# Dilated attention in a fused decoder trunk: far keys handled class by class, shorter score blocks, and a reordered state-space output

## The chip, the cores and the metric

The kernel runs on one core of one Trainium2 chip. The metric is the device time of one execution in microseconds (us). The kernel before took 2345.99 us, the median of three runs from 2345.98 to 2347.3. The profiled execution, from which all rows below come, took 2347.55 us; its span from the first to the last instruction is 2345.70 us.

## The reference

Two layers of a decoder trunk on a sequence of 1024 tokens and 1024 features, all in float32. Layer 0 mixes tokens with a diagonal state-space model (S5) and a gated linear unit, layer 1 with dilated attention; each is followed by a SwiGLU feed-forward block. The change touches the S5 output and the attention of layer 1:

```python
DIL_PATTERNS = ((128, 1), (512, 4), (2048, 16))     # (window, dilation); 16 heads of 64
def dilated_mixer(xn, w_qkv, w_o, cos, sin):
    q, k, v = ...                                    # projections; rotary on the first 16 of 64
    for window, dilation in DIL_PATTERNS:
        o, l = dilated_branch(q, k, v, window, dilation)   # softmax over keys at distance d,
        ...                                          # 0 <= d <= window, d % dilation == 0
    w = jax.nn.softmax(jnp.stack(lses, axis=0), axis=0)
    o = jnp.einsum('gbsh,gbshd->bshd', w, jnp.stack(outs, axis=0))
    return o.reshape(bsz, seq, D_MODEL) @ w_o
```

The three branches, joined by their softmax denominators, are the same as one causal softmax in which a key at distance d has the weight c(d), the number of patterns that contain d: every d up to 128 counts once, a multiple of 4 up to 512 once more, a multiple of 16 up to 2048 once more. Both kernels use this form. A key with c = 0 takes no part, so beyond distance 128 only keys of the query's own class mod 4 matter, and beyond 512 only those at a multiple of 16.

## The kernel before, in words

All large products are done three times over, as high part times high part, low times high and high times low, with float32r operands (`mm3`, L243 to L246). The stages follow one another: S5 and its gate, feed-forward of layer 0, attention, its output projection, feed-forward of layer 1.

In the attention stage the 16 heads are taken as 8 pairs. For each pair `qk_pair` projects queries and keys (8 token tiles, 24 matmuls of 128x256 each), `rope` turns them on GpSimd, and 128x128 transposes (L1358) bring them to the layout features by tokens, as `QH`, `QL`, `KH`, `KL`, with one head on partitions 0 to 63 and the other on 64 to 127. `v_group` projects the values of two pairs. `unit(p, gq, ...)` does the attention of the 256 queries of group gq of pair p, as two blocks of 128 queries:

- Scores (L1402). Block i is multiplied with all keys from 0 to its end, 128(i+1) keys, in steps of at most 512. Each step is three products for each of the two heads; the two heads use different halves of the array's rows.
- Mask and maximum (L1419). VectorE adds `lc`, a table with 8 log c(d) or minus infinity, and takes the row maximum; ScalarE then takes the exponential in place with the row sum into `den` (L1430).
- Product with the values. For each block of 128 keys: 4 transposes of the weights (L1448), ScalarE copies them as `ph`, VectorE makes the rest `pl` (L1461), and L1480 multiplies both with the values into `po`. The step at the diagonal has one query block (2 transposes) only.
- ScalarE and VectorE add the two halves of `po` into the tile `o` (L1504).

`finish` takes the reciprocal of `den`, spreads and transposes it for each half of the tokens (4 transposes L1528), multiplies `o`, splits it and stores it for the output projection.

The order of all instructions is laid down by a planner, the class `Steps`. Each op has an engine, a cost in us, a due time, ops that it depends on, and slots that it takes and gives back ("sc": 2 score banks, "pt": 2, "po": 2, "t2": 4 tiles for `ph` and `pl`, "z" and "s": large tiles). It walks through time and gives each free engine the ready op that is due first. The hardware then runs each engine's queue in that order, held only by semaphores. For the seventh pair (p = 7) there is nothing left to project; parts of the output projection (`opart`, L244 to L246 into `po_`) are put in between where their banks are free.

In S5, `y_ops` (eight times, t = 0 to 7) adds in two PSUM banks `Y[0]` and `Y[1]` first 16 products of 128 rows (L741), then 32 products of 64 rows (L745): all of the lower row half (e = 0), then all of the upper (e = 1).

Of the kernel before, what the change touches and what calls it, by code (L numbers as in the profile page):

```python
# [39 lines left out]
SL = 12.0  # L40
# [30 lines left out]
def shape_constants():  # L71
    ident = np.eye(128, dtype=np.float32)
    i16 = np.tile(np.eye(16, dtype=np.float32), (8, 1))
    p = np.arange(128)[:, None]
    u = np.arange(1024)[None, :]
    delta = p + 896 - u
    c = ((delta >= 0) & (delta <= 128)).astype(np.float64)
    c += (delta >= 0) & (delta % 4 == 0) & (delta <= 512)
    c += (delta >= 0) & (delta % 16 == 0) & (delta <= 2048)
    lc = np.where(c > 0, 8.0 * np.log(np.maximum(c, 1.0)), NEG).astype(np.float32)  # L80
    inv = (np.float32(ROPE_THETA) ** (-np.arange(0, 16, 2, dtype=np.float32) / np.float32(16))).astype(np.float32)
    inv = np.broadcast_to(inv[None, :], (128, 8))
    return {"cst": np.ascontiguousarray(np.concatenate([ident, i16, inv], axis=1)), "lc": lc}
# [87 lines left out]
def trunk(tc, a, out):  # L171
# [39 lines left out]
    cst = const.tile([128, 152], F32, name="cst")  # L211
    ident, i16, inv = cst[:, 0:128], cst[:, 128:144], cst[:, 144:152]
    vec = const.tile([128, 56], F32, name="vec")
# [518 lines left out]
    def y_ops(t, at_, sd_, us, gs, tdep):  # L732
# [3 lines left out]
        def mm():  # L736
# [5 lines left out]
            for e in range(2):  # L742
                for q in range(4):
                    for ri in range(2):
# [9 lines left out]
        o = op("pe", 5.2, at_, mm, sd_ + tdep, take=["ey"], give=["b", "b", "b", f"sst{pb}"])  # L754
# [465 lines left out]
    sch = Steps({"z": 14, "s": 6, "nat": 2, "t2": 4, "tx": 2, "raw": 2, "w": 3, "sc": 2, "pt": 2, "po": 2, "qk": 2, "mx": 6}, ids={"s": [0, 0, 0, 0, 1, 1]})  # L1220
# [106 lines left out]
    def qk_pair(p, a0, a1):  # L1327
# [9 lines left out]
        for hf in range(2):  # L1337
            evs = []
            for tau in range(4 * hf, 4 * hf + 4):
# [8 lines left out]
                evs.append(op(ACT_, c_act(256, 1, 1), at_ + span, ev, [l, rso], take=["nat"] if tau % 4 == 0 else [], give=[t["bank"]]))  # L1348
# [26 lines left out]

    def unit(p, gq, a_s, a_t, a_e, last, pair):
# [6 lines left out]
        if "den" not in pair:  # L1383
            pair["den"] = am.tile([128, 2, 8], F32, tag="den", name=uid("den"), bufs=2)
        blk = [{}, {}]
        exps = []
        for b in range(2):
            i = 2 * gq + b
            n = 128 * (i + 1)
            wide = n > 512  # L1390
            t = blk[b]
            t["s"], t["mx"] = [None, None], [None, None]
            ms_ = [[], []]
            for c0 in range(0, n, 512):
                w = min(512, n - c0)

                def sc(t=t, i=i, c0=c0, w=w):
                    t[c0] = [bank(psc, "sc") for _ in range(2)]
                    qs = slice(128 * i, 128 * i + 128)
# [4 lines left out]
                o = op(PE_, max(0.64, 0.00135 * w), a_s + 0.01 * b, sc, qdeps, take=["sc", "sc"],  # L1404
                       give=["z"] * 4 if last and b == 1 and c0 + w == n else [], chain="sc")
                lasts["sc"] = o
                for h in range(2):
                    def mask(t=t, n=n, i=i, c0=c0, w=w, h=h, wide=wide):
                        if c0 == 0:
                            if wide or h == 0:  # L1410
                                tl = Z4("s_") if sch.got["s"] else B4("s_")
                                if not wide:
                                    t["s"] = [half(tl, 0), half(tl, 1)]
                                else:
                                    t["s"][h] = tl
                            t["mx"][h] = am.tile([128, 3], F32, tag="mx", name=uid("mx"), bufs=6)
                        mx = t["mx"][h]
                        l0 = 896 - 128 * i + c0
                        V.tensor_tensor_reduce(t["s"][h][:, c0:c0 + w], t[c0][h][:, 0:w], lc[:, l0:l0 + w], op0=ALU.add, op1=ALU.max,  # L1419
                                               scale=1.0, scalar=-3.0e38, accum_out=mx[:, c0 // 512:c0 // 512 + 1])  # L1420
                        if n <= 512:
                            V.tensor_scalar(mx[:, 2:3], mx[:, 0:1], -0.125, None, op0=ALU.mult)
                        elif c0:
                            V.tensor_scalar(mx[:, 2:3], mx[:, 0:1], mx[:, 1:2], -0.125, op0=ALU.max, op1=ALU.mult)
                    tk = (["mx"] + (["s"] if wide or h == 0 else [])) if c0 == 0 else []
                    ms_[h].append(op(DVE_, c_dve(w) + (0.15 if c0 + w == n else 0), a_s + 0.5, mask, [o] + ms_[h][-1:],
                                     take=tk, give=["sc"], chain="mask"))
            for h in range(2):
                def ex(t=t, n=n, i=i, h=h):
# [336 lines left out]
```

## Time and profile before

| what | value |
|---|---|
| median of three runs | 2345.99 us |
| profiled execution | 2347.55 us |
| its span | 2345.70 us |
| TensorE (PE) busy | 2255.6 us, 96% |
| VectorE (DVE) busy | 1482.9 us, 63% |
| ScalarE (ACT) busy | 962.4 us, 41% |
| GpSimd (POOL) busy | 761.0 us, 32% |
| bytes moved | 185.73 MB, mean 79 GB/s |

A busy share says how long at least one instruction of the engine was under way. Matmuls overlap: one of 256 columns is shown with 0.28 us, but the next one starts 0.12 us after it. What a matmul costs in a full queue is therefore read from start to start in the timeline, not from its duration.

### The profile page before, as it was taken

What the parts mean: (1) busy time and instruction counts of PE and PEld (TensorE: products, weight loads), DVE (VectorE), ACT (ScalarE), POOL (GpSimd) and SP (SyncE); (2) the same over time, 40 slices, a digit from 0 to 9 for tenths busy, and PEclk for the clock granted to TensorE, in tenths of its full rate; (3) what the DMA queues carried; (4) which work ended last, traced back from release to release, by engine and by line L of the source; (5) the groups of instructions that cost most, each with busy time, mean ns of one, the idle gap of its engine ahead of it and who ended that gap; (6) DMA issues with size and microseconds to landing.
All of it is one profiled execution on the core that took longest, in us unless ns stands there. A gap on an engine that the chain in (4) does not pass through costs nothing.

```text
span 2345.7 us, 32083 instructions
## 1 busy us (share of the span) xinstructions
PE 2255.6 (96%) x12424; PEld 1908.7 (81%) x12424; DVE 1482.9 (63%) x2463; ACT 962.4 (41%) x1845; POOL 761.0 (32%) x620
## 2 busy tenths in 40 slices
PE   4779999999999999999999999989999999999998
PEld 3667888888888888889999999968788888888887
DVE  9994357866666535355676666675976667763434
ACT  7522334333322324245565656554533333332333
POOL 6661226665565301031112121011454444430100
PEclk9879999999999999999999999999999999999999
DMA  5212322222221512120111010142222222153112
GB/s 144 85 51 67 107 89 65 83 88 82 88 83 54 224 54 81 46 72 28 37 46 37 28 55 28 55 135 82 72 91 89 91 81 81 54 185 138 46 54 90
DMA packets 203931, 185.73 MB, mean 79 GB/s; under 512 B 18697, under 2 KB 171521, under 8 KB 203778
## 3 DMA queue, kind: packets, MB, share of 16 engines
q1 hardware_dynamic: 201762, 176.34, 23.4%
q0 software_dynamic: 2016, 7.34, 0.9%
q8 instruction: 98, 1.61, 0.3%
q14 instruction: 55, 0.45, 0.1%
HBM read 141.71 MB, written 41.94 MB: 78 GB/s over the span
## 4 chain that ended last, share of the span: by engine, by line
PE 87%; DVE 7%; ACT 2%; DMA 1%; POOL 1%; issue 1%; SPq 0%; POOLq 0%; DVEq 0%; ACTq 0%
PE pT L246 7%; PE pT L245 7%; PE pT L244 7%; PE pB L245 5%; PE pB L244 5%; PE pB L246 5%; PE pqk L244 4%; PE pqk L246 4%; PE pqk L245 4%; PE fin L244 3%; PE fin L245 3%; PE fin L246 3%; PE po L1480 3%; PE dn L244 3%; PE dn L245 3%; PE dn L246 3%
## 5 line engine op out<-in xcount | busy, mean ns | idle before, releaser
L244 PE MATMUL pqk<-whi,hh 128*128 128x256 f32 x768 | 228.4, 297 | 0.4 <-ACT nat L1346 0.4
L246 PE MATMUL pqk<-whi,hl 128*128 128x256 f32 x768 | 217.0, 283 | 0.8 <-DVE hl L1105 0.8
L245 PE MATMUL pqk<-wlo,hh 128*128 128x256 f32 x768 | 217.0, 283 | 0.0
L246 PE MATMUL pT<-T,S 128*128 128x512 f32 x528 | 205.7, 390 | 0.9 <-DVE S L990 0.9
L244 PE MATMUL pT<-T,S 128*128 128x512 f32 x528 | 205.9, 390 | 0.6 <-ACT T L209 0.5
L245 PE MATMUL pT<-T,S 128*128 128x512 f32 x528 | 205.8, 390 | 0.4 <-DVE T L895 0.4
L1085 DVE TENSOR_TENSOR dwl<-wraw,dwh 128x512 fp32r<-128x512 f32 x86 | 64.5, 754 | 216.7 <-ACT dwh L209 206.8
L990 DVE TENSOR_TENSOR A<-wraw,A 128x512 fp32r<-128x512 f32 x132 | 139.4, 1068 | 77.1 <-ACT A L209 76.5
L209 ACT ACTIVATE dwh<-wraw 128x512 fp32r<-128x512 f32 x86 | 53.6, 629 | 265.4 <-PE dn L245 133.9
L244 PEld LDWEIGHTS pqk<-whi,hh 128*128 128x128 f32 x768 | 146.4, 191 | 9.9 <-issue 8.1
L246 PEld LDWEIGHTS pqk<-whi,hl 128*128 128x128 f32 x768 | 146.3, 191 | 1.0 <-DVE hl L1105 1.0
L1461 DVE TENSOR_TENSOR pl<-ptp,ph 128x512 fp32r<-128x512 f32 (+1 forms) x160 | 100.1, 634 | 74.2 <-ACT ph L209 73.4
L245 PEld LDWEIGHTS pqk<-wlo,hh 128*128 128x128 f32 x768 | 146.7, 191 | 0.0
L244 PE MATMUL pB<-B,A 128*128 128x512 f32 x352 | 137.5, 391 | 0.0
L245 PE MATMUL pB<-B,A 128*128 128x512 f32 x352 | 137.2, 390 | 0.0
L246 PE MATMUL pB<-B,A 128*128 128x512 f32 x352 | 137.1, 390 | 0.0
L245 PE MATMUL dn<-sl,dwh 128*128 128x512 f32 x352 | 136.7, 389 | 0.0
L244 PE MATMUL dn<-sh,dwh 128*128 128x512 f32 x352 | 135.5, 390 | 1.0 <-DVE dtmp L1099 1.0
L246 PE MATMUL dn<-sh,dwl 128*128 128x512 f32 x352 | 134.8, 389 | 0.0
L245 PE MATMUL fin<-dwl,sh 128*128 128x512 f32 x336 | 130.8, 389 | 0.0
L209 ACT ACTIVATE A<-wraw 128x512 fp32r<-128x512 f32 x132 | 80.4, 624 | 120.8 <-DMA wraw<-in_ffn_w_gate_up_dram 72.8
L246 PE MATMUL fin<-dwh,sl 128*128 128x512 f32 x336 | 129.7, 389 | 0.0
(1137 smaller groups left out, 6221.3 us busy)
## 6 DMA issues: line engine op xcount, KB each, us to landing
wraw<-in_ffn_w_gate_up_dram SPq DMA_DIRECT2D x88, 512.0 KB, 3.9
wraw<-in_ffn_w_down_dram SPq DMA_DIRECT2D x44, 512.0 KB, 3.3
hidd<-hid SPq DMA_DIRECT2D x32, 512.0 KB, 2.8
hd<-hidd SPq DMA_DIRECT2D x32, 512.0 KB, 8.9
wraw<-in_s_w_glu_dram SPq DMA_DIRECT2D x16, 512.0 KB, 4.0
wraw<-in_dil_w_qkv_dram SPq DMA_DIRECT2D x32, 256.0 KB, 3.3
x<-in_x_dram SPq DMA_DIRECT2D x8, 512.0 KB, 7.3
xts<-xT SPq DMA_DIRECT2D x8, 512.0 KB, 3.3
```

The lines of the kernel that those rows point to most:

```text
L209: A.activation(o, i, AF.Copy)
L244: T.matmul(ps, lh, rh, start=first, stop=False)
L245: T.matmul(ps, lh, rl, start=False, stop=False)
L246: T.matmul(ps, ll, rh, start=False, stop=last)
L990: V.tensor_sub(half(t, 1), src, half(t, 0).bitcast(F32))
L1085: V.tensor_sub(wl, half(raw, i), wh.bitcast(F32))
L1461: V.tensor_sub(o_, i_, (t["ph"][:, :, 1] if part else t["ph"]).bitcast(F32))
L1480: T.matmul(o_, l_, r_[:, h, cs], start=x == 0 and n_ == 0, stop=x == len(js) - 1 and n_ == len(todo) - 1)
```

## The change

Attention, in `unit`: blocks 4 to 7 (the second half of the tokens) get near keys only. `first_key` gives the first key block, 0 for blocks 0 to 3, 3 for block 4 and 4 for blocks 5 to 7. So the blocks have 128, 256, 384, 512, 256, 256, 384 and 512 keys. The two blocks of a group share one score step when both together have at most 512 keys (groups 0 and 2). The steps of the value product are `[0, 1]`, `[0, 1, 3, 2]`, `[4, 3, 5]` and `[4, 5, 7, 6]`; in groups 0 and 2 the first step's low part is multiplied last ("held").

A new function `far` handles, for each pair, the 512 queries of the second half with the keys of the first half at a distance over 128: in four classes mod 4, 128 queries by 128 keys each. Queries and keys of a class are read with a stride of 4 elements. The values are gathered by class with 8 DMAs from GpSimd's queue. The far part has a maximum and a sum of its own; `join` spreads them from class order to token order with one matmul, and finds the factors for both parts; `finish` then scales both parts of the second half and adds them. The due times share out the same 49 us per pair among five parts instead of four, the "z" slots go from 14 to 15 and the "s" slots from 6 to 5. The evacuations of the projections (L1346) stay in order (a chain).

S5, in `y_ops`: the 32 products of L745 alternate between the two row halves, and their planned cost goes from 5.2 to 4.0 us.

```diff
@@ y_ops @@
-            for e in range(2):
-                for q in range(4):
-                    for ri in range(2):
+            for q in range(4):
+                for ri in range(2):
+                    for e in range(2):
                         T.matmul(Y[e][:, q], sd[64 * e:64 * e + 64, ri, q, 0:128],
...
-        o = op("pe", 5.2, at_, mm, sd_ + tdep, take=["ey"], give=["b", "b", "b", f"sst{pb}"])
+        o = op("pe", 4.0, at_, mm, sd_ + tdep, take=["ey"], give=["b", "b", "b", f"sst{pb}"])
@@ unit @@
+        ids_ = [2 * gq, 2 * gq + 1]
+        first = [first_key(i) for i in ids_]
+        ns = [128 * (i + 1 - f) for i, f in zip(ids_, first)]
+        steps = [(0, 1)] if sum(ns) <= 512 else [(0,), (1,)]
...
+                for b in st_:
+                    i, k0, n = ids_[b], 128 * first[b], ns[b]
                     for x, (q_, k_) in enumerate((("QH", "KH"), ("QL", "KH"), ("QH", "KL"))):
                         for h in range(2):
-                            T.matmul(t[c0][h][:, 0:w], qk[q_][own[h], qs], qk[k_][own[h], c0:c0 + w], start=x == 0, stop=x == 2)
+                            T.matmul(bk["p"][h][:, c0:c0 + n], qk[q_][own[h], 128 * i:128 * i + 128], qk[k_][own[h], k0:k0 + n],
+                                     start=x == 0, stop=x == 2)
...
-        js = list(range(2 * gq)) + ([2 * gq + 1, 2 * gq] if gq else [0, 1])
+        js = ([0, 1], [0, 1, 3, 2], [4, 3, 5], [4, 5, 7, 6])[gq]
+        held = gq % 2 == 0
...
+                if held:
+                    todo = [(j, 1)] if x == 0 else [(j, 1), (j, 0)] + ([(js[0], 2)] if end else [])
...
+            give = [] if held and x == 0 else ["t2"] * (4 if held and end else 2)
@@ far (new) @@
+        def cls(ap, c, base):
+            return ap[:, base:base + 512].rearrange("d (i c) -> d c i", c=4)[:, c]
+        def load():
+            t["v"] = Z4(f"vc{p}", F32R, (128, 2, 4, 128))
+            for h in range(2):
+                for tau in range(4):
+                    nc.gpsimd.dma_start(t["v"][32 * tau:32 * tau + 32, h], vv[h]["v"][:, tau].rearrange("k a d -> k (a d)"))
+        vl = op(POOL_, 6.0, a_s - 12, load, vends[:4], take=["z"])
+        def sc():
+            t["p"] = [bank(psc, "sc") for _ in range(2)]
+            for c in range(4):
+                for x, (q_, k_) in enumerate((("QH", "KH"), ("QL", "KH"), ("QH", "KL"))):
+                    for h in range(2):
+                        T.matmul(t["p"][h][:, 128 * c:128 * c + 128], cls(qk[q_][own[h]], c, 512), cls(qk[k_][own[h]], c, 0),
+                                 start=x == 0, stop=x == 2)
...
+                for c in range(4):
+                    cs = slice(128 * c, 128 * c + 128)
+                    V.tensor_tensor_reduce(t["s"][h][:, cs], t["p"][h][:, cs], lc[:, 768:896], op0=ALU.add, op1=ALU.max, ...)
...
+                for c in range(4):
+                    sl_ = t["s"][h][:, 128 * c:128 * c + 128]
+                    A.activation(sl_, sl_, AF.Exp, bias=pair["fs"][:, 0, h, c:c + 1], scale=0.125, accum_out=pair["fs"][:, 1, h, c:c + 1])
...
+        for cp in range(2):                       # two classes a step: 4 transposes, ph, pl, then
+                for b in range(2):
+                    c = 2 * cp + b
+                    for h in range(2):
+                        o_ = po["p"][h][:, 128 * c:128 * c + 128]
+                        T.matmul(o_, t["v"][:, h, c], r["ph"][:, h, b], start=True, stop=False)
+                        T.matmul(o_, t["v"][:, h, c], r["pl"][:, h, b], start=False, stop=True)
...
+            o = op(ACT_, c_act(512), a_e, cl, [pvl], take=["tx"])
+            pair["fadd"].append(op(DVE_, c_dve(512), a_e, add, [o], give=["po", "tx"]))
@@ join (new) @@
+        o = op(DVE_, 0.15, at_, spread, pair["fexp"], chain="join")
+        o = op(PE_, 0.2, at_, mm, [o], take=["pt"])
+        o = op(DVE_, 0.7, at_, pick, [o] + pair["exps"][2] + pair["exps"][3], give=["pt"])
+        o = op(ACT_, 0.2, at_, ex, [o])
+        return op(DVE_, 0.55, at_, weigh, [o], chain="join")
@@ finish @@
+            for part in range(1 + hf):            # wide, bc (4 transposes) and mul, for each part
...
+            if hf:
+                o = op(DVE_, c_dve(512), at_ + 0.1, add, [o], give=["s"])
@@ pairs @@
-        order = (0, 1, 2, 3) if p == 0 else (3, 0, 2, 1)
-        cost = [4 * g + 3 + GC for g in order]
+        order = (0, 1, 4, 2, 3) if p == 0 else (3, 4, 0, 2, 1)
+        cost = [(3, 7, 4, 7, 4)[g] + GC for g in order]
```

## Rows read from the trace of the kernel before

**Rows 1.** Part 1 of the page: busy time, share of the span, instructions.

```profile
PE 2255.6 (96%) x12424; PEld 1908.7 (81%) x12424; DVE 1482.9 (63%) x2463; ACT 962.4 (41%) x1845; POOL 761.0 (32%) x620
```

**Rows 2.** Stretches: us; busy of PE, PEld, DVE, ACT, POOL; granted clock; DMA.

```profile
80.00:180.00 100.00, 75.36 (x547) 65.10 (x546) 93.43 (x143) 32.54 (x67) 58.22 (x44) 0.78 0.14 38
180.00:210.00 30.00, 28.45 (x207) 24.86 (x208) 13.39 (x22) 5.99 (x11) 6.62 (x6) 0.88 0.09 23
1060.00:1525.00 465.00, 464.37 (x3816) 427.10 (x3816) 301.06 (x852) 275.39 (x661) 77.82 (x104) 1.00 0.13 40
1525.00:1590.00 65.00, 55.78 (x336) 41.63 (x335) 43.24 (x114) 34.05 (x74) 9.14 (x18) 0.95 0.39 125
```

**Rows 3.** Waits of PE from 1000 to 1620 us: total us, times, longest.

```profile
PE sc L1402 <- DVE mx L1419: 4.2, 5, 3.0
PE ptqk L1358 <- POOL nat L1571: 1.2, 1, 1.2
```

**Rows 4.** Timeline of PE (start, us, instruction): a score step of 128 keys.

```profile
1284.72 0.28 PE L246 MATMUL pqk<-whi,hl 128*128 128x256 f32 x1
1284.93 0.33 PE L1402 MATMUL sc<-KH,QH 64*128 64x128 f32 x2
1285.09 0.28 PE L1402 MATMUL sc<-KH,QL 64*128 64x128 f32 x2
1285.21 0.28 PE L1402 MATMUL sc<-KL,QH 64*128 64x128 f32 x2
...
1285.63 0.28 PE L245 MATMUL pqk<-wlo,hh 128*128 128x256 f32 x1
```

**Rows 5.** Timeline of PE: around a score step of 256 and one of 512 keys.

```profile
1057.66 0.28 PE L246 MATMUL pqk<-whi,hl 128*128 128x256 f32 x1
...
1058.09 0.28 PE L1402 MATMUL sc<-KH,QL 64*128 64x256 f32 x2
1058.21 0.28 PE L1402 MATMUL sc<-KL,QH 64*128 64x256 f32 x2
...
1058.64 0.28 PE L245 MATMUL pqk<-wlo,hh 128*128 128x256 f32 x1
...
1280.33 0.28 PE L246 MATMUL pqk<-whi,hl 128*128 128x256 f32 x1
...
1281.65 0.28 PE L245 MATMUL pqk<-wlo,hh 128*128 128x256 f32 x1
```

**Rows 6.** Timeline of PE: a value product, transposes, and a value product at the diagonal.

```profile
1293.87 0.40 PE L1480 MATMUL po<-pl,v 128*64 128x256 f32 x2
...
1294.35 0.27 PE L1448 MATMUL ptp<-cst,s__1797_10999 128*128 128x128 f32 x1
1294.46 0.27 PE L1448 MATMUL ptp<-cst,s__1812_11076 128*128 128x128 f32 x1
...
1522.33 0.28 PE L1480 MATMUL po<-pl,v 128*64 128x128 f32 x2
1522.44 0.39 PE L1480 MATMUL po<-ph,v 128*128 128x128 f32 x2
1522.67 0.30 PE L1448 MATMUL ptp<-cst,s__2415_14300 128*128 128x128 f32 x1
```

**Rows 7.** Groups of DVE, 1030 to 1600 us: busy us, mean ns | idle before.

```profile
L1461 DVE TENSOR_TENSOR pl<-ptp,ph 128x512 fp32r<-128x512 f32 x128 | 86.9, 687 | 58.0 <-ACT ph L209 57.5
```

**Rows 8.** One line's instructions (L1419): ns min/median/max, first and last start.

```profile
L1419 DVE CUSTOM_DVE_ANT_0 s__1278_8079<-sc,lc x2: 280/285/290, 1056.3 to 1056.8; 128x128 f32<-128x128 f32 x2
```

**Rows 9.** Timeline of PE in S5: 32 column-half products, and the 32 of L745.

```profile
38.66 1.97 PE L669 MATMUL E<-U,P 128*64 128x128 f32 x32
...
191.12 3.50 PE L745 MATMUL Y<-GG,sst 64*128 64x128 f32 x32
```

**Rows 10.** DMA issues: KB each, us to landing; and issue time on POOL (groups).

```profile
T<-scr SPq DMA_DIRECT2D x64, 64.0 KB, 2.6
...
L1612 POOL DMA_DIRECT2D oh<-osp x7 | 4.0, 578 | 25.9 <-PE po L1480 16.1 <-PE ptp L1448 9.8
```

More of the change, by code (lines that the diff above doesn't have):

```diff
@@ L1384, in unit @@
             pair["den"] = am.tile([128, 2, 8], F32, tag="den", name=uid("den"), bufs=2)
+            pair["nm"] = am.tile([128, 2, 8], F32, tag="nm", name=uid("nm"), bufs=2)
         blk = [{}, {}]
         exps = []
[L1387 to L1399, printed above, removed]
+        ids_ = [2 * gq, 2 * gq + 1]
@@ new lines, in sc, with mask, ex @@
+                    c0 += n
+            w = sum(ns[b] for b in st_)
+            o = op(PE_, max(0.64, 0.00135 * w), a_s + 0.01 * st_[0], sc, qdeps, take=["sc", "sc"],
+                   give=["z"] * 4 if last and st_[-1] == 1 else [], chain="sc")
+            lasts["sc"] = o
+            for b in st_:
+                t, i, n = blk[b], ids_[b], ns[b]
+                t["s"] = [None, None]
+                c0 = ns[0] if len(st_) == 2 and b == 1 else 0
+                mk = [None, None]
+                for h in range(2):
+                    def mask(t=t, n=n, i=i, c0=c0, h=h, bk=bk):
+                        if h == 0:
+                            tl = Z4("s_") if sch.got["s"] else B4("s_")
+                            t["s"] = [half(tl, 0), half(tl, 1)]
+                        mx = am.tile([128, 4], F32, tag="mx", name=uid("mx"), bufs=6)
+                        l0 = 512 if i == 4 else 512 - n
+                        V.tensor_tensor_reduce(t["s"][h][:, 0:n], bk["p"][h][:, c0:c0 + n], lc[:, l0:l0 + n], op0=ALU.add, op1=ALU.max,
+                                               scale=1.0, scalar=-3.0e38, accum_out=mx[:, 0:1])
+                        V.tensor_scalar(pair["nm"][:, h, i:i + 1], mx[:, 0:1], -0.125, None, op0=ALU.mult)
+                    mk[h] = op(DVE_, c_dve(n) + 0.15, a_s + 0.5, mask, [o], take=["mx"] + (["s"] if h == 0 else []),
+                               give=["sc"] if b == st_[-1] else [], chain="mask")
+                for h in range(2):
+                    def ex(t=t, n=n, i=i, h=h):
+                        A.activation(t["s"][h][:, 0:n], t["s"][h][:, 0:n], AF.Exp, bias=pair["nm"][:, h, i:i + 1], scale=0.125,
+                                     accum_out=pair["den"][:, h, i:i + 1])
+                    exps.append(op(ACT_, c_act(n, 0, 1) + 0.09, a_s + 1, ex, [mk[0], mk[h]], give=["mx"]))
@@ L1512, in rec @@
         def rec():
-            t["rd"] = am.tile([128, 2, 8], F32, tag="rd", name=uid("rd"), bufs=2)
-            V.reciprocal(t["rd"], pair["den"])
-        r = op(DVE_, 0.12, at_, rec, [e for gq in range(4) for e in pair["exps"][gq]])
+            t["rd"] = am.tile([128, 2, 4], F32, tag="rd", name=uid("rd"), bufs=2)
+            V.reciprocal(t["rd"], pair["den"][:, :, 0:4])
+        r = op(DVE_, 0.12, at_, rec, [e for gq in range(4) for e in pair["exps"][gq]] + pair["fexp"])
+        jn = join(at_ - 0.5, pair)
         last = []
@@ L1550, in put @@
                 nc.sync.dma_start(os_[p, 1][:, cs], half(pair["o"], hf))
-            o = op(DVE_, 0.6, at_, wide, [r] + pair["adds"][2 * hf] + pair["adds"][2 * hf + 1], take=["tx"])
-            o = op(PE_, 0.44, at_, bc, [o] + last, take=["pt"], give=["tx"])
-            o = op(DVE_, c_dve(512), at_ + 0.1, mul, [o], give=["pt"])
             tk = ["tx"] if p < 7 else ["s"] if hf == 0 else []
@@ L1596, in trunk @@
             d = PL * cost[n_] / sum(cost)
-            unit(p, g, pos - SL, pos, pos + d, n_ == 3, pair)
+            if g == 4:
+                far(p, pos - SL, pos, pos + d, pair)
+            else:
+                unit(p, g, pos - SL, pos, pos + d, n_ == 4, pair)
             pos += d
```

227 lines of the change are left out of this document (155 added, 72 removed).

## The prediction, written before the changed kernel was run

> **What bounds the kernel now.** I read the busy shares first: PE is busy 96% of the span, no other engine over 63% [rows 1]. Then the stretches, because a mean hides the stages [rows 2]. From 1060 to 1525 us, the attention of pairs 0 to 6, PE is busy 464.37 of 465 us at full clock, DVE 301.06 and ACT 275.39: there each microsecond of TensorE work that goes is a microsecond gained, as long as DVE and ACT keep up. From 1525 to 1590 us (the end of pair 6 and pair 7, nothing left to project) PE is busy 55.78 of 65, so the chain through DVE and ACT sets part of the pace. In S5, from 80 to 180 us, DVE is busy 93.43 of 100 and PE 75.36 at a granted clock of 0.78: DVE bounds; from 180 to 210 us PE is at 28.45 of 30. Third, the waits of PE: over the whole attention the largest is 4.2 us in all, for DVE's mask [rows 3], most of it in pair 7. So the sum is one of PE time, start to start.
>
> **Scores.** Rows 4 and 5 give the cost of a step between projections: from the start of the last matmul ahead to the start of the second one behind, less two projections of 0.12 us. A step of 128 keys takes 1285.63 - 1284.72 - 0.24 = 0.67 us [rows 4], one of 256 keys 0.74, one of 512 keys 1.08 [rows 5]; one of 384 lies between, and there are two before and two after, so it drops out. Of the 0.67 us only 3 x 0.112 is the products (start of the third pair less start of the second [rows 4]); the rest is the turn from full rows to half rows and back. Three more products of 128 columns in a step that has been opened cost 0.34 us, of 256 columns 3 x 0.12 = 0.36.
>
> Before, a pair has 12 steps: two of 128, two of 256, two of 384 and six of 512, without the 384s 1.34 + 1.48 + 6.48 = 9.30 us. After: group 0 shared, 0.74 + 0.34 = 1.08; group 2 shared, 0.74 + 0.36 = 1.10; blocks 3 and 7, two of 512, 2.16; and `far`, 12 products for each head, 0.67 + 9 x 0.112 = 1.68. Together 6.02. Difference: -3.3 us a pair.
>
> The far products read both operands with a stride of 4 elements, 16 bytes. No row here has TensorE reading so. Floor: as the 128-column rows, 0.112 us a product. Ceiling: double, since a product of 128 columns hardly costs less than one of 256 (0.112 against 0.12 [rows 4, 5]): something other than the columns, 54 ns at 2.4 GHz, sets its pace. If only the moving side halves its rate, that stays hidden; if the pace itself doubles, it costs 12 x 0.112 = 1.3 us a pair, 10.8 in all. I take the floor, being the row of the same shape, and keep the ceiling as a rival. "SBUF — State Buffer" of the Trainium skill (Door 1: The DMA port swizzle) states that on-chip memory is read in lines of 16 bytes, that two hits on a line are needed for full rate, and that each access to a new line pays. By that the far products would come out at the ceiling; no row of this trace shows it either way.
>
> **Value product.** A full step costs 1294.35 - 1293.87 = 0.48 us, a diagonal one 1522.67 - 1522.33 = 0.34, a transpose 0.11 [rows 6]. Before, a pair has 17 products at full width (group 0 pads) and 3 narrow: 8.16 + 1.02 = 9.18. After: 8 full and 5 narrow, 3.84 + 1.70 = 5.54, and 16 of 128 columns in `far`, at (1522.67 - 1522.44)/2 = 0.115 us [rows 6], 1.84: 7.38. Difference -1.8. Multiplying the held low part last moves it, at the same width; it costs PE nothing, but keeps two of the four `ph`/`pl` tiles to the end of the group, so there only one step is in flight. Transposes: 72 before, 8 x 4 + 5 x 2 + 8 = 50 after, -22 x 0.11 = -2.4.
>
> **Finish and join.** Four more transposes, +0.44, and one matmul of 64 columns in `join`, between 0.11 (a transpose) and 0.27 (with half of a 0.32 us turn): +0.15. Sum for a pair: -3.3 - 1.8 - 2.4 + 0.6 = -6.9 us; for eight, -55.2.
>
> **What DVE and ACT do.** They must not get longer, since their share rises when PE's time falls. DVE loses 8 full `pl` steps and gains 2 full and one narrow, -6 x 0.687 + 0.42 = -3.7 [rows 7]. Its masks go from 4608 columns a head to 2688 near and 512 far; the far ones are 8 instructions of 0.285 [rows 8] where 128 columns more in a long one cost 0.13: about -3. It gains two 512-wide additions of the far part, one spread, one product and one addition in `finish` and some dozen tiny instructions in `join`: about +5.5. Net -1. ACT's `ph` copies shrink in the same numbers; its exponentials go from 4608 to 3200 columns a head but from 16 to 24 instructions, and two copies come in: I put it at 0. Both stay as they are while a pair's PE time falls from 61 to 54 us: DVE from 65% to 72%, ACT from 59% to 66%. That isn't full, but less slack: I add +2 for stalls, bounds 0 and +8.
>
> The edits of order and slots (evacuations in a chain, an exponential that waits for the mask of head 0 too, which DVE does first anyway, one "z" more and one "s" less with only two "s" held by a unit instead of up to four) I cost at nothing: the planner fits other ops around them, and what they could cost is inside the stalls' bounds.
>
> **Class-ordered values.** 8 DMAs of 64 KB a pair on POOL's queue; issuing one took 0.58 us, and 64 KB landed in 2.6 us [rows 10]. POOL is busy 77.82 of 465 us [rows 2], 8 x 0.58 = 4.6 us more a pair fits. The load is due 24 us ahead of its use (12 ahead of the score, which is 12 ahead of the product). Behind it on POOL stand the scaling of weights and the rotary. Nothing while it overlaps; bounds 0 and the rival below.
>
> **Pair 7.** There the chain counts: score step, mask, exponential, transposes, `ph`, `pl`, product. It gets shorter too (7 score steps for 12, 15 value steps for 20), but has one more handing over of the `po` banks and a longer finish: three rounds of spread, transpose, multiply for two, each some 2 us, mostly covered by parts of the output projection. I count 5 of its 6.9 us: +1.9, bounds 0 and +6.9.
>
> **S5 output.** The 32 products of L745 take 3.5 us, one after another; 32 products of 128 columns that alternate between halves of the array take 1.97 [rows 9]; score pairs on the two row halves start together [rows 4]. So alternating saves some 1.6 us for each of 8. The last two (from 189 and 203 us) lie where PE is full [rows 2]: -3.2. The six before lie beside a full DVE; there PE time is mostly not the end. I take -5 in all, bounds 0 and -16 (ten for the six, more at the lower clock).
>
> **Sum.** -55.2 + 2 + 1.9 - 5 = -56.3. The profiled execution took 2347.55 us (span 2345.70 and 1.85 around it): 2291.2; the median of the runs is 1.56 us below it: 2289.7. Forecast **2290 us**, with its own bounds 2272 (S5 -16, no stall) to 2304 (stall +8, pair 7 no gain).
>
> **Rivals.**
> 1. The far products run at half pace: +10.8, **2301 us**. For: the stride, and no row that clears it. Against: at 128 columns the columns don't set the pace.
> 2. DVE and ACT become the bound in pairs 0 to 6: the score-to-product chain lags, the projections run out, PE waits. Then the gain is what the busier engine loses, about 1 us of DVE a pair, and S5's 5: **2333 us**. For: an even pair, without values to project, has only about 47 us of PE time after. Against: 65% and 59% now, and a trace where PE waits for nearly nothing.
> 3. Slower: GpSimd's queue stands. It issues in order; when the tile for the class-ordered values isn't free, or 8 x (0.58 + 2.6) = 25 us of loads run one after another instead of overlapped, the rotary behind them comes late, and the next pair's transposes wait as they did once for 1.2 us [rows 3]. It turns the result when PE waits more than 56/8 = 7 us a pair. With 9 us a pair: -56 + 72 = +16, **2362 us**. Against: POOL is busy only a sixth of the time, and the load has 24 us.
> 4. The alternation of Y gives nothing, because it lies beside DVE: +5, inside the forecast's bounds.
>
> **Chances.** Forecast 0.66, half pace 0.14, DVE and ACT bound 0.12, POOL 0.08. The range takes in the first two with their bounds, 2272 to 2320; the other two are left out. Faster by over 0.2% (4.7 us, about what a measurement of this kernel can tell from no change): the first three, less a little for cases between the second rival and none: 0.89. Within 0.2%: 0.03. Slower: 0.08.
>
> **What would show it.** Right: PE still full from 1060 us on, no wait of PE over some 5 us in all before pair 7; a shared step of 256 + 256 keys at 1.1 us; 12 far products 0.11 us apart; 32 products of Y in about 1.9 us. Wrong: far products 0.22 apart (rival 1); PE idle with the releaser `pl` or `mx` in pairs 0 to 6 (rival 2); `ptqk` or the far `po` waiting for POOL or a DMA (rival 3). If pairs 0 to 6 gain 7 us each and the total doesn't, the loss is in pair 7's stretch.

## The result, and the profile after

The changed kernel took 2310.89 us (median of four runs, 2307.26 to 2311.3); the kernel before, run beside it, 2346.64 us (four runs). The ratio is 0.9844, with a 95% interval of 0.9827 to 0.9861: 1.6% faster, 35.8 us where the prediction had 56. The time lies within the predicted range, 2272 to 2320 us, but 21 us above the forecast of 2290, and 7 us above the 2304 that the forecast had as its own upper bound: it is inside because the range also took in rival 1. The profiled execution is the fastest of the four, 2307.26 us with a span of 2305.4. One execution, of v_from_sp below, took 2494.23 us at a mean granted clock of 0.841 where all others show 0.978 to 0.988; it counts in that kernel's median (2307.29 without it) but not in its ratio.

Part 1 of the page of the kernel after, the line that answers to [rows 1]: busy time, share, instructions.

```profile
PE 2198.3 (95%) x12200; PEld 1871.8 (81%) x12200; DVE 1466.8 (64%) x2559; ACT 945.5 (41%) x1949; POOL 794.4 (34%) x684
```

Stretches of the kernel after (columns as in [rows 2]): S5, its end, pairs 0 to 6, pair 7.

```profile
80.00:180.00 100.00, 59.67 (x568) 49.43 (x567) 96.00 (x145) 31.52 (x68) 59.20 (x45) 0.80 0.14 39
180.00:210.00 30.00, 30.00 (x220) 25.74 (x220) 15.53 (x24) 7.43 (x12) 5.35 (x5) 0.93 0.16 42
1026.00:1490.00 464.00, 456.93 (x3822) 435.47 (x3821) 296.10 (x953) 275.73 (x778) 127.08 (x182) 0.99 0.18 51
1490.00:1560.00 70.00, 66.01 (x396) 54.26 (x396) 47.10 (x144) 34.68 (x92) 9.05 (x18) 0.93 0.41 129
```

The stretch of [rows 2] from 1060 us leaves out the first 28 us of pairs 0 to 6. Equal work, from the first projection to the last, is this, first before, then after:

```profile
1032.30:1525.30 493.00, 491.10 (x4034) 452.66 (x4033) 316.17 (x882) 289.10 (x687) 93.53 (x118) 1.00 0.13 40
1026.30:1491.40 465.10, 458.03 (x3833) 436.64 (x3832) 296.69 (x954) 275.68 (x777) 126.78 (x182) 0.99 0.18 51
```

PE is still what bounds pairs 0 to 6: 458 of 465 us, beside DVE's 297 and ACT's 276. Two things are new there. PE has 7.1 us without work where it had 1.9, and the granted clock is 0.99 where it was 1.00.

The stages are bounded by the first and last start of a tile's instructions. The tile view of the kernel before (ns min/median/max; then first and last start in us): projections of queries and keys, `finish`'s transposes, the last feed-forward product.

```profile
L244 PE MATMUL pqk<-whi,hh x768: 277/283/388, 1032.3 to 1525.1; 128*128 128x256 f32 x192
L1528 PE MATMUL prd<-cst,rdw x64: 270/273/328, 1146.2 to 1593.4; 128*128 128x128 f32 x64
L246 PE MATMUL fin<-dw,sl x16: 388/389/390, 2319.1 to 2338.2; 128*128 128x512 f32 x16
```

The same of the kernel after:

```profile
L254 PE MATMUL pqk<-whi,hh x768: 277/283/415, 1026.3 to 1491.1; 128*128 128x256 f32 x192
L1682 PE MATMUL prd<-cst,rdw x96: 270/272/476, 1135.5 to 1552.1; 128*128 128x128 f32 x96
L256 PE MATMUL fin<-dw,sl x16: 388/389/389, 2276.3 to 2295.3; 128*128 128x512 f32 x16
```

From such rows comes the table on which the rest of this text hangs (us; "last projection" is the last start of the projections' third product, 0.2 to 0.3 us behind the row shown). The right two columns are experiments told of below: the far products read without a stride, and three remedies together.

| stretch | before | after | after - before | forecast | no stride | remedies |
|---|---|---|---|---|---|---|
| start to the first projection | 1032.3 | 1026.3 | -6.0 | -5 | 1025.6 | 1027.4 |
| first to last projection (pairs 0 to 6) | 493.0 | 465.1 | -27.9 | -46.3 | 452.4 | 448.8 |
| to the last transpose of `finish` (pair 7) | 68.1 | 60.7 | -7.4 | -5 | 60.2 | 63.2 |
| to the last product of the last layer | 744.8 | 743.2 | -1.6 | 0 | 743.3 | 742.3 |
| to the end of the span | 7.5 | 10.1 | +2.6 | 0 | 10.1 | 7.5 |
| sum | 2345.7 | 2305.4 | -40.3 | -56.3 | 2291.6 | 2289.2 |

(The forecast of the second row is seven pairs at -6.9 and the 2 us of stalls.) So the miss has a place: 18.4 us in pairs 0 to 6 and 2.6 at the very end, against which 5 us more than expected came from the other rows. The table explains 16 of the 21 us by which the forecast was missed. Of the rest, 3.6 are the distance from the profiled execution to the median (the other three show a mean granted clock of 0.980 or 0.981 for its 0.983), and 1.6 were taken off the forecast because the median before lay under the profiled one. Single traces scatter, too: with the same S5 code the first projection starts between 1025.6 and 1030.3 us in the twelve traces of the changed kernel and those made from it.

Timeline of PE in the kernel after: a step of 128 and 256 keys together; the start of a far step with two of its projections ahead; the 32 products of Y.

```profile
1049.45 0.28 PE L256 MATMUL pqk<-whi,hl 128*128 128x256 f32 x1
1049.66 0.33 PE L1416 MATMUL sc<-KH,QH 64*128 64x128 f32 x2
...
1050.34 0.28 PE L1416 MATMUL sc<-KL,QH 64*128 64x256 f32 x2
1050.55 0.39 PE L254 MATMUL pqk<-whi,hh 128*128 128x256 f32 x1
1050.77 0.28 PE L255 MATMUL pqk<-wlo,hh 128*128 128x256 f32 x1
...
1075.29 0.28 PE L255 MATMUL pqk<-wlo,hh 128*128 128x256 f32 x1
1075.41 0.28 PE L256 MATMUL pqk<-whi,hl 128*128 128x256 f32 x1
1075.62 0.49 PE L1543 MATMUL sc<-KH,QH 64*128 64x128 f32 x2
1075.93 0.41 PE L1543 MATMUL sc<-KH,QL 64*128 64x128 f32 x2
1076.16 0.41 PE L1543 MATMUL sc<-KL,QH 64*128 64x128 f32 x2
1076.40 0.41 PE L1543 MATMUL sc<-KH,QH 64*128 64x128 f32 x2
...
201.03 2.06 PE L755 MATMUL Y<-GG,sst 64*128 64x128 f32 x32
```

The shared step costs 1050.77 - 1049.45 - 0.24 = 1.08 us, by the way of counting of [rows 4], and the forecast had 1.08. Y's products take 2.06 us for 3.50 [rows 9], forecast 1.9. But the far products start 0.23 us apart (1076.16 to 1076.40), and over all eight far steps the median is 0.233: twice the 0.112 of [rows 4].

Waits of PE from 1000 to 1620 us in the kernel after, the three largest (columns as in [rows 3]):

```profile
PE ptqk L1368 <- POOL nat L1736: 5.7, 6, 1.1
PE prd L1682 <- DVE QL L1379: 1.4, 1, 1.4
PE sc L1416 <- DVE mx L1436: 1.3, 2, 1.1
```

The transposes of queries and keys wait six times for GpSimd, 5.7 us in all, where there was one such wait of 1.2 us [rows 3]. That gives three suspects: the stride, the granted clock, and GpSimd.

### The profile page after: what moved, and what is told of

Its sections match the earlier page's. It is cut to its first block, busy times and chain, and to the rows that moved or that the text cites. A ratio compares the mean times of both kernels' runs of the same rounds, so it can differ in the third digit from the quotient of the medians.

```text
span 2305.4 us, 32010 instructions
## 1 busy us (share of the span) xinstructions
PE 2198.3 (95%) x12200; PEld 1871.8 (81%) x12200; DVE 1466.8 (64%) x2559; ACT 945.5 (41%) x1949; POOL 794.4 (34%) x684
## 4 chain that ended last, share of the span: by engine, by line
PE 85%; DVE 8%; POOL 2%; ACT 2%; DMA 1%; issue 1%; SPq 0%; DVEq 0%; POOLq 0%; ACTq 0%
PE pT L256 7%; PE pT L254 7%; PE pT L255 7%; PE pB L255 5%; PE pB L254 5%; PE pB L256 5%; PE pqk L254 4%; PE pqk L256 4%; PE pqk L255 4%; PE fin L254 3%; PE fin L255 3%; PE fin L256 3%; PE dn L254 3%; PE dn L255 3%; PE dn L256 3%; PE glu L254 2%
## 5 line engine op out<-in xcount | busy, mean ns | idle before, releaser
L1000 DVE TENSOR_TENSOR A<-wraw,A 128x512 fp32r<-128x512 f32 x132 | 138.2, 1060 | 76.6 <-ACT A L218 76.1
L254 PE MATMUL fin<-dwh,sh 128*128 128x512 f32 x336 | 127.6, 389 | 1.4 <-ACT dwh L218 1.4
```

The costliest lines, as they stand in the source:

```text
L254: T.matmul(ps, lh, rh, start=first, stop=False)
L1000: V.tensor_sub(half(t, 1), src, half(t, 0).bitcast(F32))
```

## Experiments

### The stride: which side of the product pays

Four kernels differ from the changed one in one line, the far scores. Their far products work on other keys or queries than the reference's, at the same count and size.

```diff
-  T.matmul(..., cls(qk[q_][own[h]], c, 512), cls(qk[k_][own[h]], c, 0), ...)
+  T.matmul(..., qk[q_][own[h], 512 + 128 * c:640 + 128 * c], qk[k_][own[h], 128 * c:128 * c + 128], ...)   # far_contig
+  T.matmul(..., qk[q_][own[h], 512 + 128 * c:640 + 128 * c], cls(qk[k_][own[h]], c, 0), ...)               # far_kstride
+  T.matmul(..., cls(qk[q_][own[h]], c, 512), qk[k_][own[h], 128 * c:128 * c + 128], ...)                   # far_qstride
+  T.matmul(..., cls2(qk[q_][own[h]], c), cls(qk[k_][own[h]], c, 0), ...)                                   # far_stride2
+  # cls2: two sets of 256 queries, two classes in each: a stride of 2 elements in place of 4
```

> The changed kernel, but the far products read queries and keys as four contiguous blocks of 128 in place of four classes with a stride of 4 elements (so it attends to other far keys than the reference: the far part of the result is left wrong). Theory (the stride sets the pace of the 12 far products of a pair): in the changed kernel they stand 0.233 us apart; here 0.11 to 0.12, and 8 x 12 x 0.117 = 11 us are gained, about 2300 us. Rival (something else holds them, such as twelve products opened one after another on half rows): they stay 0.23 apart and the time stays at 2311.

> As far_contig, but only the queries (the loaded, stationary side) are read contiguous; the keys (the moving side) keep the stride of 4. The far part of the result is left wrong in the same way. If the load of the stationary side sets the pace, the far products stand 0.11 to 0.12 us apart as in far_contig; if the moving side does, 0.23; if both do in sum, between.

> The other half: only the keys (moving) are read contiguous, the queries (stationary) keep the stride of 4. The far part of the result is left wrong. If the load of the stationary side sets the pace, 0.23 us apart; if the moving side, 0.11 to 0.12.

> The changed kernel with the stationary queries of the far products read with a stride of two elements (8 bytes) instead of four (16 bytes): two sets of 256 queries, each in two classes, stand in the place of one set of 512 in four. The far part of what it computes is another one than the reference's; the keys keep their stride of four, and the work is of the same size. The Trainium skill (SBUF - State Buffer, Door 1: The DMA port swizzle) speaks of 16-byte lines that give the full pace if two elements of each are used. By that rule the far products stand 0.11 to 0.12 us apart and the time is that of contiguous queries, 2294 to 2300 us. Rival: any stride other than one halves the pace of the stationary side; then they stand 0.23 us apart and the time is 2307 to 2311 us. A step of 0.17 us would say that the cost goes by the bytes that are passed over.

The first operand (queries) is the one that is loaded into the array, the second (keys) streams past. Measured, with the median of the start-to-start times of the far products:

| kernel | queries | keys | far products apart | time, us |
|---|---|---|---|---|
| after | stride 4 | stride 4 | 0.233 | 2310.89 |
| far_contig | 1 | 1 | 0.112 | 2294.92 (2293.44 to 2297.17) |
| far_kstride | 1 | 4 | 0.118 | 2296.62 (one run) |
| far_qstride | 4 | 1 | 0.234 | 2311.23 (one run) |
| far_stride2 | 2 | 4 | 0.120 | 2294.83 (one run) |

The kernel before took 2346.62 us beside the three far kernels in the middle and 2344.92 beside far_stride2. far_contig's ratio to the kernel before is 0.9782 (0.9767 to 0.9797); its 16 us are more than the 11 expected, and the next part has the rest. Two of its far products in the timeline:

```profile
1075.42 0.28 PE L1543 MATMUL sc<-KH,QH 64*128 64x128 f32 x2
1075.53 0.28 PE L1543 MATMUL sc<-KH,QL 64*128 64x128 f32 x2
```

The line view of the weight loads (PEld) of far scores shows where the time sits: ns min/median/max, first and last start. First the kernel after, then far_kstride, far_qstride and far_stride2.

```profile
L1543 PEld LDWEIGHTS sc<-KH,QL x64: 306/327/328, 1075.8 to 1505.6; 64*128 64x128 f32 x64
```

```profile
L1543 PEld LDWEIGHTS sc<-KH,QL x64: 186/195/330, 1077.8 to 1496.0; 64*128 64x128 f32 x64
```

```profile
L1543 PEld LDWEIGHTS sc<-KH,QL x64: 308/327/329, 1079.9 to 1509.8; 64*128 64x128 f32 x64
```

```profile
L1547 PEld LDWEIGHTS sc<-KH,QL x64: 192/193/328, 1075.5 to 1493.8; 64*128 64x128 f32 x64
```

The load of 128 columns takes 0.33 us with a stride of four elements and 0.19 with two or one; the stride of the keys does nothing to it. Rival 1 had come true, and only by the loaded side. On the streaming side a halved rate could still be there: 512 columns take 0.225 us start to start (the gate's products, at 197 us of the kernel after), so 128 are worth 56 ns (an estimate), and twice that, 112, is no more than the load needs anyway. These runs can't tell.

The Trainium skill, "SBUF — State Buffer" (Door 1: The DMA port swizzle), asks for two hits on each line of 16 bytes; by that a stride of 8 bytes is free and one of 16 is not. Both agree here: 0.120 and 0.233. The same passage goes on to say that four float32 elements can be strided for free; the 0.233 of this stride speaks against that.

The Trainium skill, "TensorE: Matmul & The Clock Gate" (LDWEIGHTS (loading the stationary operand)), states that a load takes its number of columns divided by 1.2, in ns, however many rows it has. For 128 columns that is, as an estimate, 107 ns, and the 0.112 us between the products of far_contig lies near it.

### The clock behind a strided step

The stretch from 1026 to 1490 us had a clock of 0.99. Cut finer, around the first far step of the kernel after (same columns; the clock is the third number from the end):

```profile
1070.00:1075.00 5.00, 5.00 (x46) 5.00 (x45) 1.51 (x7) 2.48 (x10) 3.26 (x7) 1.00 0.30 54
1075.00:1078.00 3.00, 3.00 (x26) 2.87 (x27) 1.88 (x6) 0.79 (x3) 3.00 (x6) 1.00 0.73 132
1079.00:1081.00 2.00, 2.00 (x11) 2.00 (x11) 1.83 (x18) 1.11 (x6) 0.00 (x0) 0.50 0.24 38
1082.00:1084.00 2.00, 2.00 (x19) 2.00 (x18) 0.23 (x1) 1.98 (x10) 0.00 (x0) 1.00 0.00 0
```

And the timeline of PE there:

```profile
1080.06 0.41 PE L256 MATMUL pqk<-whi,hl 128*128 128x256 f32 x1
1080.28 0.41 PE L254 MATMUL pqk<-whi,hh 128*128 128x256 f32 x1
...
1082.04 0.28 PE L254 MATMUL pqk<-whi,hh 128*128 128x256 f32 x1
1082.16 0.28 PE L255 MATMUL pqk<-wlo,hh 128*128 128x256 f32 x1
```

While the far products run, 0.23 us apart, the records show PE without a gap and at 2.4 GHz. At their end the granted clock falls to 1.2 GHz, and the projections behind them stand 0.22 us apart instead of 0.12 until it is given back. The same stretch around that step in q_by_class (next section), which reads its queries without a stride:

```profile
1077.00:1080.00 3.00, 3.00 (x37) 2.73 (x36) 2.57 (x12) 0.88 (x3) 3.00 (x7) 1.00 0.72 131
1080.00:1084.00 4.00, 4.00 (x36) 4.00 (x35) 1.70 (x15) 3.40 (x17) 0.79 (x2) 1.00 0.33 54
```

I summed the time at 1.2 GHz from the clock of each stretch of 4 us between 1040 and 1484 us (a clock of 0.80 over 4 us is 1.6 us at half speed). In the kernels with far products 0.233 us apart: after 10.3 us (behind three of its first seven far steps), the same kernel once more 13.6 (four), far_qstride 10.3, v_from_sp 13.7, rope_cost 6.8, no_sharing 17.0 (five). In those with 0.112 to 0.120, far_contig, far_kstride, far_stride2, q_by_class, q_by_class_s4 and combined, and in the kernel before: none. That is a fall behind 21 of 42 such steps, against none of 42. Idle time of PE alone doesn't set it off: far_contig has the same 5.7 us of waits for the rotary and 8.7 us without work in pairs 0 to 6, more than the 7.1 of the kernel after, and no fall, while rope_cost has 2.5 us without work and two falls. So the stride costs a second time, half of those microseconds: 5.2 in the profiled execution of the kernel after, 3.4 to 8.5 in the others. A second way of counting agrees: PE's busy time in pairs 0 to 6 is 458.0 us in the kernel after and 443.7 in far_contig, 14.3 us apart, of which the far products explain 9 to 10. Why it comes behind some of the equal steps and not behind others stays open; I have no run that varies it. It fits that one kernel's executions lie up to 8 us apart, but only the profiled ones show where their clock fell.

### Removing the stride: the queries laid out by class

q_by_class copies the 512 queries of the second half class by class right after they have left PSUM, high part by ScalarE, low part by VectorE, into a "z" tile. q_by_class_s4 gives that tile a slot of its own, "z" 16 and "s" 4.

```diff
+                    if hf and not x:
+                        t_["QC"] = Z4(f"QC{p}", F32R, (128, 2, 512))
+                        copy(by_class(t_["QC"][:, 0], False), by_class(t_["QH"][:, cs].bitcast(F32), True))
...
-  T.matmul(..., cls(qk[q_][own[h]], c, 512), cls(qk[k_][own[h]], c, 0), ...)
+  T.matmul(..., qk["QC"][own[h], int(q_ == "QL"), 128 * c:128 * c + 128], cls(qk[k_][own[h]], c, 0), ...)
```

> The changed kernel, computing all of it, with a copy of the second half's queries in class order (ScalarE copies the high part, VectorE the low part, each 512 columns a pair, into one large tile more out of the 15 slots), so that the far products load a contiguous stationary side; the keys keep their stride. Theory (only the stationary side's stride costs): far products 0.11 to 0.12 us apart, 11 to 14 us gained less some 0.5 us of ACT and DVE a pair that PE hides: 2297 to 2302 us. Rival (the two copies and the held tile cost the chain as much as the stride did): 2308 to 2312 us.

> The same with one tile moved from the score slots (5 to 4) to the large slots (15 to 16), so the copy takes no slot from the projections. If the slot was what held q_by_class back, this is faster by some us; if four score tiles are too few, slower. Theory: 2297 us.

Measured: 2297.87 us, ratio 0.9800 (0.9784 to 0.9817), far products 0.118 apart; with the other slots 2299.7, ratio 0.9812 (0.9797 to 0.9826), no difference that can be told. The copies (medians of 1.16 us of ScalarE and 0.64 of VectorE a pair) cost little: far_kstride, the same without them, has 0.9787 to the kernel before beside it, in one run; up to some 3 us can't be told from nothing here.

### GpSimd: the queue or the plan

v_from_sp moves the loads of the class-ordered values from GpSimd's queue to SyncE's, in the plan too (4.0 us of SyncE for 6.0 of GpSimd). rope_cost leaves them and changes the plan alone: the rotary work, planned at 1.9 us, takes six instructions of 0.46, 0.46, 0.46, 0.46, 0.73 and 0.49 us on average, 3.0 together; it is now planned at 3.6.

```diff
-                    nc.gpsimd.dma_start(t["v"][32 * tau:32 * tau + 32, h], vv[h]["v"][:, tau].rearrange("k a d -> k (a d)"))
+                    nc.sync.dma_start(t["v"][32 * tau:32 * tau + 32, h].bitcast(F32), ...)                                      # v_from_sp
...
-            r = op(POOL_, 1.9, at_ - 2, lambda hf=hf: rope(nat[hf]["n"], hf), evs, take=["tx"], give=["tx"])
+            r = op(POOL_, 3.6, at_ - 2, lambda hf=hf: rope(nat[hf]["n"], hf), evs, take=["tx"], give=["tx"])                    # rope_cost
```

> The changed kernel with the 8 loads of class-ordered values of each pair issued from SyncE's queue instead of GpSimd's. Theory of the third rival of the prediction (the loads hold up GpSimd's rotary): PE's waits for the rotary go from 5.7 us to the 1.2 us of before, 4 us gained, 2307 us. Rival (the rotary is late by its own length): waits unchanged, 2311 us.

> The changed kernel with one number of the planner changed: the rotary's cost on GpSimd from 1.9 to 3.6 us, about what it took in the changed kernel's trace, so that the transposes that need it are put later in PE's queue. In the changed kernel PE waited 5.7 us in six places for that step. Theory (a planned cost that is too short): these waits go, 4 to 6 us gained, 2306 us. Rival (the wait only moves): same, 2311 us.

v_from_sp took 2307.91 us, ratio 0.984 (0.9823 to 0.9856): no difference. Its largest wait of PE, 1000 to 1620 us:

```profile
PE ptqk L1368 <- POOL nat L1736: 5.7, 6, 1.1
```

With the loads out of the queue the wait stands, to the tenth. rope_cost took 2300.67 us, ratio 0.9816 (0.9801 to 0.983). Its largest waits:

```profile
PE prd L1682 <- DVE QL L1379: 2.6, 1, 2.6
PE po L1596 <- DVE o L1516: 1.4, 2, 1.1
```

The wait for the rotary is gone, and another took 1.2 us of it back. So it was not the queue but the plan: the planner put the transposes 1.1 us too early, and PE stood. The gain of 7 to 10 us (6.6 by the ratios) is more than the expected 4 to 6; this trace also has 6.8 us at 1.2 GHz for 10.3 to 13.6, worth 2 to 3. Whether that is the plan's doing or chance is open.

v_from_sp shows something else, at the very end of the span. The closing DRAIN on GpSimd in the kernel after (ns min/median/max), then in v_from_sp:

```profile
L1930 POOLq DRAIN  x3: 40/98/7049, 2297.5 to 2305.1; - x3
```

```profile
L1930 POOLq DRAIN  x3: 40/98/1821, 2301.5 to 2306.5; - x3
```

It takes 7.05 us where GpSimd has issued 78 DMAs and 1.82 where it has issued 14, though the last of them was issued hundreds of microseconds before. From the last product to the end of the span it is 10.1 us in the one and 7.6 in the other. The kernel before issued 14 there too, with a DRAIN of 1.82 us and 7.5 us to the end. That is the table's +2.6.

### Y alone

The kernel before, with nothing of the change but the order of Y's products and their planned cost.

```diff
-            for e in range(2):
-                for q in range(4):
-                    for ri in range(2):
+            for q in range(4):
+                for ri in range(2):
+                    for e in range(2):
...
-        o = op("pe", 5.2, at_, mm, sd_ + tdep, take=["ey"], give=["b", "b", "b", f"sst{pb}"])
+        o = op("pe", 4.0, at_, mm, sd_ + tdep, take=["ey"], give=["b", "b", "b", f"sst{pb}"])
```

> The kernel before with the alternation of Y's 32 products and their planned cost alone. Theory (as predicted, some 5 us, of which the last two groups give 3): the projections of the attention stage start 5 to 6 us earlier, 2346.6 - 6 = 2341 us. Rival (beside a full VectorE it gives nothing): 2346 us.

Measured 2343.24 us against 2346.62, ratio 0.9988 (0.9978 to 0.9997), ten runs: 0.7 to 5.2 us, less than the 5 to 6 expected. In its trace the projections of the attention start at 1025.6 us for 1032.3; part of that is given back behind, the span is 5.5 us shorter.

### Sharing undone

```diff
-        steps = [(0, 1)] if sum(ns) <= 512 else [(0,), (1,)]
+        steps = [(0,), (1,)]
...
-                c0 = ns[0] if len(st_) == 2 and b == 1 else 0
+                c0 = 0
```

> The changed kernel with the sharing of score steps undone: the blocks of 256 and of 128 keys of a group each have a step of their own again. My theory: a score step costs a fixed time beside its products (a step of 128 keys stood for 0.67 us though its three products are worth 0.34 us, a step of 256 keys for 0.74), so each pair gets two more of those fixed parts, 2 x 0.33 = 0.7 us, 8 pairs 5 to 6 us: 2312 to 2317 us, all of it in the start-to-start sum of the score products. Rival 1: the exponential and the copies behind a step are what the next step waits for; then more and smaller steps also lengthen these, by about 0.3 us a step on ScalarE, and 10 us and more come out. Rival 2: the fixed part lies under work of VectorE and ScalarE anyway and the time is that of the unaltered kernel within 1 us.

It ran beside the changed kernel once more:

> The changed kernel once more, unaltered, as the measure for the three that stand beside it on this chip: 2307 to 2311 us, far score products 0.233 us apart.

after_again took 2308.7 us (2307.38 to 2315.68), ratio 0.9853 (0.9838 to 0.9868); no_sharing 2319.64 (2318.55 to 2320.98), ratio 0.9894 (0.9881 to 0.9908). That is 10.9 us by the medians, 5.2 by the spans of the two profiled executions (2313.8 and 2319.0). Timeline of PE in no_sharing, the two steps of group 0 apart:

```profile
1051.54 0.28 PE L256 MATMUL pqk<-whi,hl 128*128 128x256 f32 x1
1051.75 0.33 PE L1416 MATMUL sc<-KH,QH 64*128 64x128 f32 x2
...
1052.46 0.28 PE L255 MATMUL pqk<-wlo,hh 128*128 128x256 f32 x1
...
1053.64 0.28 PE L256 MATMUL pqk<-whi,hl 128*128 128x256 f32 x1
1053.85 0.39 PE L1416 MATMUL sc<-KH,QH 64*128 64x256 f32 x2
...
1054.63 0.28 PE L255 MATMUL pqk<-wlo,hh 128*128 128x256 f32 x1
```

Counted as before: 0.68 and 0.75 us, 1.43 for the 1.08 of the shared step. The turn's price of 0.35 us is as I had it, and the second rival (hidden) falls. In the attention the two traces differ by 6.5 us, 4.1 of them in the score products start to start and 1.7 in the clock (17.0 against 13.6 us at 1.2 GHz). Theory and first rival are told apart by no more than that: the trace speaks for the turns, the medians lie 3 us above what the theory allows and would fit the rival. The clock is a candidate for the difference: over whole executions its mean is 0.978 or 0.979 in no_sharing, and 0.981 in the profiled execution of after_again but 0.982 or 0.983 in the other three, whose falls no trace shows.

### The three remedies together

combined has the copy of the queries, the rotary planned at 3.6 us and the value loads on SyncE, as in the diffs above.

> The changed kernel with the three remedies together: the 512 far queries of a half are laid out class by class in a copy when they leave PSUM, so that the stationary side of the far scores is read without a stride; the planner counts 3.6 us for the rotary work on GpSimd instead of 1.9; the values of the classes are loaded from SyncE's queue instead of GpSimd's. My theory is that each loss has its own cause, so the gains add up: far products 0.118 us apart (about -11 to -13 us), no TensorE wait of the query-key transposes on the rotary result (about -5 to -10 us, as the planner alone gave), and the end of the program 2.5 us earlier. From 2307 to 2311 us that makes 2283 to 2294 us. Rival: the copy and the later rotary slots take each other's places in the plan (VectorE and ScalarE do the copies between the same products), and the sum ends where the copy alone did, at 2297 to 2300 us.

Measured 2287.84 us (2286.22 to 2290.95), ratio to the kernel before 0.9758 (0.9744 to 0.9771); beside it, on the same chip, after_again with 0.9853. It beats both kernels, 57 us below before and 21 below the changed one. Its stretch of pairs 0 to 6 (with 14 us of pair 7: its last projection starts at 1476 us), and its largest wait of PE from 1000 to 1620 us:

```profile
1026.00:1490.00 464.00, 456.01 (x3903) 431.75 (x3902) 316.57 (x995) 290.54 (x800) 99.99 (x128) 1.00 0.19 58
```

```profile
PE po L1503 <- DVE pl L1483: 2.4, 3, 0.9
```

The clock is whole again, no wait for GpSimd is left, and the far products stand 0.118 us apart. The three gains add up. The runs come from different chips, on which the kernel before took 2343.95 to 2346.64 us, so I compare ratios to the kernel before beside each, at 2345 us: from 0.9844 to 0.9800 for the copy is 10.3 us, to 0.9816 for the plan 6.6, with 2.5 for the end 19.4; combined, at 0.9758, gained 20.2 (22.3 from after_again's 0.9853). Each ratio is good to some 4 us. The rival, that they take each other's places and the sum ends at 2297 to 2300 us, falls.

## Why the prediction was right or wrong

**The number: inside by the width of the range.** The forecast's own case did not come; rival 1 did, to which the prediction gave 0.14, and with more beside it than its 2301 us. The bounds of the forecast don't come out of the terms named with them: 2289.7 - 11 - 2 is 2276.7 for 2272, and 2289.7 + 6 + 5 is 2300.7 for 2304; for 2320 there is no working at all. Two of the prediction's own signs of being wrong showed: far products 0.23 us apart, and the transposes of queries and keys waiting for GpSimd, 5.7 us where it allowed some 5 in all.

**What bounds the kernel: right.** PE time set pairs 0 to 6 before and after. DVE's and ACT's busy time there fell from 316.2 to 296.7 us and from 289.1 to 275.7, 2.8 and 1.9 us a pair, where the prediction had 1 and 0; so their shares did not rise. Rival 2 didn't come; no wait on `pl` or `mx` is over 1.3 us in the kernel after.

**Near scores, value product, transposes: right.** Start to start over the attention, the value products lost 14.1 us (forecast 8 x 1.8 = 14.4) and the transposes of the weights 19.7 (19.2). The shared step cost its 1.08 us. All scores lost 11.5 us where 26 was forecast; with the stride gone, in far_contig, 22.3, and the projections, in whose start to start a part of each turn is counted, 3.7 more when their waits are left out.

**Far products: wrong, the term was mis-sized.** The step of the prediction that failed is "I take the floor, being the row of the same shape". The row had the shape but not the access. 12 products at 0.233 instead of 0.112 cost 1.45 us a pair, 11.6 in all; rival 1 had 10.8 and 2301 us. My argument against it, that the columns don't set the pace at 128, was true and beside the point: what sets the pace there is the load of the other operand, and that was the side that the stride slowed. The ceiling, not the floor, was the value to take, or the queries to be copied.

**The clock: not in the prediction.** 10.3 us at 1.2 GHz behind three strided steps cost 5.2 us in the profiled execution. No rival had it.

**Stalls: mis-sized.** I added 2 us; PE's idle time in pairs 0 to 6 rose from 1.9 to 7.1, by 5.2 (inside the bounds of 0 to 8), and most of it is the wait for the rotary, 5.7 us for 1.2. I looked for it in GpSimd's queue (rival 3, which didn't come) when it was the planned cost of 1.9 us for some 3 us of work. The rotary was as slow in the kernel before, six instructions of 3.1 us together; why PE hardly waited for it there I haven't shown.

**The sum for pairs 0 to 6.** Far products 7 x 1.45 = 10.2, clock 5.2, stalls 5.2 - 2 = 3.2: 18.6 us, and the table has 18.4. With all three removed, combined stands at 448.8 us there, 44.2 below before for a forecast of 46.3, and at 2289.2 in span for the forecast's 2345.7 - 56.3 = 2289.4. That last agreement is partly luck: 2.1 us are missing in pairs 0 to 6, and 2.5 came in the stretch behind the attention, where nothing had been changed.

**S5 and pair 7: right, a little small.** -6.0 us for -5 up to the first projection, within a scatter of some 5 us among traces; the runs of Y alone, 0.7 to 5.2 us faster, show that a gain comes from there, and rival 4 falls, though not by much. Pair 7's stretch gained 7.4 for 5, and PE has 66 of 70 us there.

**The class-ordered values: a cost in a place I hadn't looked at.** The loads ran beside other work, as costed, and then lengthened the end of the program by 2.6 us.

## What to carry to other kernels

When a matmul reads an operand with a stride, ask first which side it is: the loaded side set the pace of a 128-column product here, and 16 bytes doubled it where 8 bytes didn't. A bound from a row of the same shape holds only if the row reads its operands in the same way. Where a planner lays out the queues, compare each planned cost with the measured duration of the op, because an optimistic one turns into a stall of the engine that is full.

## What the runs showed of the hardware that I had not expected

- The granted clock fell to 1.2 GHz with PE shown busy in every record: in all six traces with far products 0.233 us apart (6.8 to 17.0 us of pairs 0 to 6), in none of the six with 0.112 to 0.120, and not in the kernel before.
- GpSimd's closing DRAIN takes 7.05 us after 78 DMAs issued there in the course of the program, and 1.82 after 14 (in the kernel before, v_from_sp and combined); with the long one the program ends 2.5 us later.
